# Seven tile products for eight in two of eight row-tile pairs of the plain down products, with weight chunks of 2048

## The chip, the cores and the metric

The kernel runs on one core of a Trainium2 chip. The metric is the device time of one execution in microseconds (us); the profile gives, for one execution of its own, the span from the first to the last instruction of the core.

## The reference

The reference is a decoder trunk of two layers on 256 tokens of 2048 features in float32. Layer 0 mixes tokens by a causal pooling mixer, layer 1 by a dilated attention with three head groups; each layer ends with a squared-relu MLP, and each of the four sublayers with a scaled residual and a layer norm:

```python
for i in range(DEPTH):                       # DEPTH = 2
    if i % N_MIXERS == 0: h = pool_mixer(x, ...)
    else:                 h = dilated_attention(x, ...)
    x = layer_norm(DEEPNORM_ALPHA * x + h, ln_mix_g[i], ln_mix_b[i])
    x = layer_norm(DEEPNORM_ALPHA * x + sqrelu_mlp(x, mlp_w_up[i], mlp_w_down[i]), ln_mlp_g[i], ln_mlp_b[i])

def sqrelu_mlp(x, w_up, w_down):             # w_up 2048 x 8192, w_down 8192 x 2048
    h = jax.nn.relu(x @ w_up)
    return (h * h) @ w_down
```

The two MLPs hold most of the work. In the kernel each product is made of three matmuls on parts of reduced width: high times high, high times low and low times high.

## The kernel before

**Weights.** All weights are planned as one list of chunks in the order of use; a chunk is 128 rows by 1024 columns (`CHUNK`). `load` (L116) gives each chunk one of 4 `raw` buffers (`RAWS`) and a DMA on SP's queue. `prefetch` (L129) then splits it by `split_from` (L61): ACT copies the high part `wh` (L62), DVE subtracts it to make `wl` (L63). A split pair sits in one of 8 buffers (`SPLITS`) until TensorE (PE) has used it. A raw buffer is free for the next DMA when DVE has made `wl`. `weights()` (L140) takes the next pair and first writes the splits of the chunks up to 8 ahead into the programs of ACT and DVE. The programs of PE, DVE and ACT are in the order in which the code is written, and each engine goes through its own in order; SP does too, and runs ahead as raws come free.

**The MLP** (L520) goes in four parts c of 2048 hidden columns. A part first makes its hidden columns in *up blocks* (`feature_major`, L186) of 512 columns, four a part (in c=0 the first is split in two of 256 columns, made by `opening` while the norm is being finished, and one block of 256). A block of 512 uses 8 chunks and four of the 8 PSUM banks, one for each 128 columns. The *hidden chain* then works on each pair of banks: ACT copies the low half out (`low`, L230), DVE adds (`u`, L231), ACT takes relu (L531) and square (L533) and makes `hH`, DVE makes `hL` (L63). Eight hidden pairs `hs[0]` to `hs[7]`, of two row tiles each, are the left operand of the part's *down products*. Parts c=0 to 2 are *plain*: four groups of 512 output columns, each by `token_major` (L248) in two banks, one for each of the two token tiles t, then added to the residual `xz` (L569, L571). Part c=3 is a `closing`, which makes the norm's moments, transposes the result and lets the next `opening` begin.

In c=0, `drain()` puts a *restore* behind a block: four DVE instructions (L352, L353) that apply the norm's gain and bias to `xz`, and the DMAs of the next rows `gb`, which POOL issues (L346).

**Start.** The pooling mixer's first product, w_in, goes in four blocks n=0 to 3 of 512 columns; behind each the windows are summed (`win`, `pv`) and split to `pT`. While n=0 runs, ACT and DVE also split the transposed input `xT`, and `feature_major` prefetches less far ahead (L195).

Of the kernel before, what the change touches and what calls it, by code (L numbers as in the profile page):

```python
# [9 lines left out]
F32 = mybir.dt.float32  # L10
# [3 lines left out]
OP = mybir.AluOpType  # L14
# [18 lines left out]
MASKED = -1e30  # L33
CHUNK = 1024
RAWS = 4
SPLITS = 8
RESIDENT = 4
MLP_PARTS = 4
UP_FIRST = (256, 256, 512, 512, 512)
UP_REST = (512, 512, 512, 512)  # L40
# [6 lines left out]
def trunk(ctx: ExitStack, tc: tile.TileContext, x, pool_w_in, pool_w_group, pool_scale, pool_w_out,  # L47
# [27 lines left out]

    def plan(w, k0, nk, n0, ncols):
        step = CHUNK // ncols
        for k in range(k0, k0 + nk, step):
            chunks.append((w[:, k:k + step, n0:n0 + ncols], step, ncols))

    def plan_columns(w, k0, nk, n0, widths):
        for ncols in widths:
            plan(w, k0, nk, n0, ncols)
            n0 += ncols

    def plan_mlp(l):
        for c in range(MLP_PARTS):
            plan_columns(w_up[l], 0, KT, c * D, UP_FIRST if c == 0 else UP_REST)
            plan_columns(w_down[l], c * KT, KT, 0, CLOSING if c == MLP_PARTS - 1 else UP_REST)

# [3 lines left out]
    def plan_values(sp):  # L94

        w_v = w_qkv.rearrange("p k (y g n) -> p k y g n", y=3, g=GROUPS)
        for k in range(0, KT, 2):
            chunks.append((w_v[:, k:k + 2, 2, 1:3, sp * 256:(sp + 1) * 256], 2, 512))

    plan_columns(w_in, 0, KT, 0, UP_REST)  # L100
    for g in range(4):
# [9 lines left out]
    plan_mlp(1)  # L111

    raws, ready = [], []
    state = {"raw": 0, "split": 0, "used": 0}

    def load(upto):  # L116

        while state["raw"] < min(upto, len(chunks)):
            src, step, ncols = chunks[state["raw"]]
            raw = wraw.tile([P, step, ncols], F32, tag="raw", name="raw")  # L120
            if len(src.shape) == 4:
                for j in range(step):
                    nc.sync.dma_start(raw[:, j, :].rearrange("p (g n) -> p g n", g=src.shape[2]), src[:, j])
            else:
                nc.sync.dma_start(raw, src)
            raws.append(raw)
            state["raw"] += 1

    def prefetch(upto):  # L129

        while state["split"] < min(upto, len(chunks)):
            load(state["split"] + 1)
            _, step, ncols = chunks[state["split"]]
            hi = wsplit.tile([P, step, ncols], F32R, tag="wh", name="wh")
            lo = wsplit.tile([P, step, ncols], F32R, tag="wl", name="wl")
            split_from(hi, lo, raws.pop(0))
            ready.append((hi, lo))
# [127 lines left out]
    def tile_products(ps, t, nk, parts, act, start=True, between=()):  # L265

        k = 0
        for i, (hi, lo) in enumerate(parts):
# [7 lines left out]
            k += step  # L276


    class Norm:
        def __init__(self, g, b, cidx, last=None):  # L280
# [58 lines left out]
        def restores(self):  # L339
# [18 lines left out]
            return [lambda n=n: restore(n) for n in range(NG)]  # L358

        def centre(self, t, ns):  # L360
            for n in ns:
                z = xz[:, t, n * 512:(n + 1) * 512]
                nc.vector.scalar_tensor_tensor(z, z, self.mv[t][:, 0:1], self.last[:, 0, n * 512:(n + 1) * 512],
                                               op0=OP.subtract, op1=OP.mult)

        def output(self, t, ns):
            for n in ns:
                sl = slice(n * 512, (n + 1) * 512)
                z = xz[:, t, sl]
# [66 lines left out]
    def opening(norm, ncols):  # L436
# [83 lines left out]
    def mlp(norm_in, norm):  # L520
        with ExitStack() as ph:
            hp = ph.enter_context(tc.tile_pool(name="hp", bufs=8))
            hb = ph.enter_context(tc.tile_pool(name="hb", bufs=2))
            if norm.last is not None:
                for i, v in enumerate((norm.g, norm.b)):
                    nc.gpsimd.dma_start(norm.last[:, i, :], v[None, :].to_broadcast([P, D]))

            def hidden(ps):
# [7 lines left out]
            def split_hidden(q):  # L536
# [3 lines left out]
                return hH, hL  # L540

            for c in range(MLP_PARTS):
                hs = []
# [19 lines left out]
                if c < MLP_PARTS - 1:  # L563
                    for n in range(NG):
                        ps = token_major(KT, 512, act)
                        for t in range(NT):
                            z = xz[:, t, n * 512:(n + 1) * 512]
                            if c == 0:
                                nc.vector.scalar_tensor_tensor(z, z, ALPHA, ps[t], op0=OP.mult, op1=OP.add)  # L569
                            else:  # L570
                                nc.vector.tensor_add(z, z, ps[t])  # L571
                else:
# [7 lines left out]
    with ExitStack() as ph:  # L580
# [127 lines left out]
        for sp in range(SLOTS // 2):  # L708
# [69 lines left out]
```

## Time and profile before

| | us |
|---|---|
| median of three runs | 2146.16 (2145.59 to 2147.05) |
| the profiled execution | 2146.52 |
| span of the profiled execution | 2144.7 |
| TensorE (PE) busy | 2124.7 (99%) |
| VectorE (DVE) busy | 1283.4 (60%) |
| ScalarE (ACT) busy | 1052.8 (49%) |

Some 1.8 us of the profiled execution lie outside its span. A busy share is an average over stages; PE is busy nearly throughout, so what counts for the time is how many matmuls it has and whether their operands and banks are ready.

### The profile page before, as it was taken

How to read it: one execution, taken by the hardware profiler on the slowest of the kernel's cores; microseconds unless marked ns; L12 is line 12 of the kernel's file. 1: busy time of each engine (PE TensorE's matmuls, PEld its weight loads, DVE VectorE, ACT ScalarE, POOL GpSimd, SP SyncE). 2: the span in 40 equal slices, each digit the busy share in tenths (PEclk: the TensorE clock that was granted, in tenths of full speed). 3: DMA queues.
4: the chain of work that ended last, by engine and by line, in shares of the span. 5: the costliest groups of instructions: out<-in, count | busy, mean ns of one | idle time of the engine just before them, and what ended most of it. 6: DMA issues, size and time to landing. Idle time of an engine off the chain costs nothing.

```text
span 2144.7 us, 29773 instructions
## 1 busy us (share of the span) xinstructions
PE 2124.7 (99%) x11745; PEld 1845.9 (86%) x11745; DVE 1283.4 (60%) x1558; ACT 1052.8 (49%) x1368; POOL 23.0 (1%) x52
## 2 busy tenths in 40 slices
PE   8999999999999999999999999999999999999998
PEld 7889888888888888898998988888888888888887
DVE  6785756555455555578656565676655555554555
ACT  4563655454355355354545444455545534644541
POOL 1000000000000000001000000000000000000000
PEclk9999999999999999999999999999999999999999
DMA  7565567556655655548555555456665566566562
GB/s 239 204 216 177 169 204 237 175 199 201 191 185 196 194 172 206 194 139 237 173 175 161 176 162 173 164 164 218 209 221 178 201 197 188 176 207 186 181 207 94
DMA packets 256045, 404.67 MB, mean 189 GB/s; under 512 B 13104, under 2 KB 109984, under 8 KB 255648
## 3 DMA queue, kind: packets, MB, share of 16 engines
q1 hardware_dynamic: 253472, 394.31, 56.7%
q0 software_dynamic: 2432, 8.45, 1.9%
q8 instruction: 92, 1.51, 0.3%
q14 instruction: 49, 0.40, 0.1%
HBM read 400.61 MB, written 2.10 MB: 188 GB/s over the span
## 4 chain that ended last, share of the span: by engine, by line
PE 96%; DVE 2%; DMA 1%; ACT 1%; issue 0%; SPq 0%; DVEq 0%; ACTq 0%
PE pt L245 45%; PE pf L202 32%; PE pf L204 16%; PE pf L221 1%; PE pq L658 1%; PE po L697 1%; DMA raw<-in_attn_w_qkv 0%; DVE wl L63 0%; PE ptr L321 0%; DMA xz<-in_x 0%; ACT xv L330 0%; DVE xT L337 0%; DVE vL L63 0%; PE ptr L458 0%; DVE xT L336 0%
## 5 line engine op out<-in xcount | busy, mean ns | idle before, releaser
L63 DVE TENSOR_TENSOR wl<-raw,wh 128x1024 fp32r<-128x1024 f32 x744 | 898.2, 1224 | 621.1 <-ACT wh L62 607.1
L62 ACT ACTIVATE wh<-raw 128x1024 fp32r<-128x1024 f32 x744 | 773.4, 1057 | 805.8 <-PE pt L245 351.4
L202 PE MATMUL pf<-xT,wh 128*128 128x512 f32 x3008 | 947.6, 396 | 0.0
L204 PEld LDWEIGHTS pf<-xT,wl 128*128 128x128 f32 x3008 | 566.0, 188 | 134.0 <-DVE wl L63 0.6
L204 PE MATMUL pf<-xT,wl 128*128 128x256 f32 x3008 | 592.2, 278 | 0.0
L202 PEld LDWEIGHTS pf<-xT,wh 128*128 128x128 f32 x3008 | 459.5, 189 | 0.5
L245 PE MATMUL pt<-wl,hH 128*128 128x512 f32 (+1 forms) x1088 | 407.0, 377 | 0.0
L245 PE MATMUL pt<-wh,hH 128*128 128x512 f32 (+1 forms) x1088 | 407.0, 377 | 0.0
L245 PE MATMUL pt<-wh,hL 128*128 128x512 f32 (+1 forms) x1088 | 398.2, 377 | 0.0
L245 PEld LDWEIGHTS pt<-wl,hH 128*128 128x128 f32 x1088 | 204.8, 188 | 37.6 <-DVE wl L63 0.4
L245 PEld LDWEIGHTS pt<-wh,hH 128*128 128x128 f32 x1088 | 204.8, 188 | 37.5
L245 PEld LDWEIGHTS pt<-wh,hL 128*128 128x128 f32 x1088 | 199.6, 188 | 37.1
L245 PE MATMUL pt<-wh,xT 128*128 128x256 f32 (+1 forms) x704 | 156.4, 314 | 1.9 <-DVE xT L336 1.5
L245 PEld LDWEIGHTS pt<-wh,xT 128*128 128x128 f32 x704 | 117.2, 191 | 10.6 <-DVE xT L336 3.1
L63 DVE TENSOR_TENSOR hL<-q,hH 128x512 fp32r<-128x512 f32 x62 | 42.9, 693 | 125.6 <-ACT hH L62 125.6
L245 PE MATMUL pt<-wl,xT 128*128 128x256 f32 (+1 forms) x352 | 106.7, 312 | 0.0
L230 ACT ACTIVATE low<-pf 128x256 f32<-128x256 f32 x188 | 61.3, 377 | 69.6 <-PE pf L204 62.7
L245 PE MATMUL pt<-wh,pT 128*128 128x512 f32 (+1 forms) x320 | 82.6, 347 | 0.0
L231 DVE TENSOR_TENSOR u<-pf,low 128x256 f32<-128x256 f32 x172 | 64.7, 418 | 26.0 <-ACT low L230 26.0
L245 PEld LDWEIGHTS pt<-wl,xT 128*128 128x128 f32 x352 | 67.2, 191 | 3.6
L531 ACT ACTIVATE r<-u 128x512 f32<-128x512 f32 x62 | 39.2, 632 | 51.0 <-DVE u L231 51.0
L245 PEld LDWEIGHTS pt<-wh,pT 128*128 128x128 f32 x320 | 56.1, 189 | 7.5
(126 smaller groups left out, 1001.8 us busy)
## 6 DMA issues: line engine op xcount, KB each, us to landing
raw<-in_mlp_w_up SPq DMA_DIRECT2D x256, 512.0 KB, 4.4
raw<-in_mlp_w_down SPq DMA_DIRECT2D x256, 512.0 KB, 4.5
raw<-in_attn_w_qkv SPq DMA_DIRECT2D x120, 512.0 KB, 4.3
raw<-in_pool_w_in SPq DMA_DIRECT2D x32, 512.0 KB, 5.4
raw<-in_pool_w_out SPq DMA_DIRECT2D x32, 512.0 KB, 4.7
raw<-in_attn_w_qkv SPq DMA_DIRECT2D x48, 256.0 KB, 3.3
raw<-in_attn_w_out SPq DMA_DIRECT2D x16, 512.0 KB, 4.4
raw<-in_pool_w_group SPq DMA_DIRECT2D x8, 512.0 KB, 5.0
```

The source lines that it names most:

```text
L62: nc.scalar.activation(hi, src, AF.Copy)
L63: nc.vector.tensor_sub(lo, src, hi.bitcast(F32))
L202: nc.tensor.matmul(ps[b], hi[:, j, sl], a, start=(k == 0), stop=False, skip_group_check=True)
L204: nc.tensor.matmul(ps[b][:, 0, :], lo[:, j, sl], a[:, 0, :], start=False, stop=(k == nk - 1), skip_group_check=True)
L221: nc.tensor.matmul(ps[b // 2][:, b % 2, :], w[:, j, sl], a[:, part, :], start=(k == 0 and i == 0 and b % 2 == 0), stop=(k == nk - 1 and i ...
L230: nc.scalar.activation(low, p[:, 1, :], AF.Copy)
L231: nc.vector.tensor_add(out[:, b, :], p[:, 0, :], low)
L245: nc.tensor.matmul(ps, a[:, sl], u, start=(start and k == 0 and i == 0), stop=(k == nk - 1 and i == 2), skip_group_check=True)
L531: nc.scalar.activation(r, ps, AF.Relu)
L658: nc.tensor.matmul(pq[:, t, :], q[u][:, b, sl], k[v][:, b, :], start=(i == 0), stop=(i == 2))
L697: nc.tensor.matmul(po, v[:, st, b * P:(b + 1) * P], p[:, g, sl], start=(i == 0), stop=(i == 3 * 2 * GROUPS - 1))
```

## The change

Two of the eight pairs of row tiles (hidden pairs 1 and 4, `SEVEN`) of each plain part are multiplied by a scheme of seven tile products where two tokens tiles times two row tiles times two column halves want eight. It needs sums of the weight's tiles (`split_seven`), sums of the hidden pair's tiles (`split_seven_left`) and sums of the products (`sums`). A plain part's down products now go in two groups of 1024 columns, with all 8 banks (`mixed_group`). Chunks are 2048 columns, with 2 raws, 4 split buffers and 2 resident chunks, which is the same memory. With chunks twice as long, the places that stand "before the last chunk" (the transposes in `closing` and `opening`) and the prefetch at the start move; `drain()` stands ahead of a block, the last norm's rows come by SP through raw buffers, and in the attention one set of transposes (not shown) stands ahead of the last value chunk.

```diff
-CHUNK = 1024
-RAWS = 4
-SPLITS = 8
-RESIDENT = 4
+CHUNK = 2048
+RAWS = 2
+SPLITS = 4
+RESIDENT = 2
+MIX = (1, 0, 2, 4, 3, 5, 6, 7)
+SEVEN = (1, 4)
...
+    def split_seven(raw):
+        q = raw.rearrange("p k (h n) -> p (k h) n", h=2)
+        t = state["diff"].tile([P, 4, 512], F32, tag="t", name="t")
+        nc.vector.tensor_sub(t[:, 0:2], q[:, 1:3], q[:, 0:1].to_broadcast([P, 2, 512]))
+        nc.vector.tensor_add(t[:, 2], q[:, 2], t[:, 0])
+        nc.vector.tensor_sub(t[:, 3], q[:, 3], t[:, 2])
+        plain, sums = split_buffers([P, 4, 512]), split_buffers([P, 4, 512])
+        split_from(plain[0][:, 1:], plain[1][:, 1:], q[:, 1:])
+        split_from(sums[0], sums[1], t)
...
-            hi, lo = weights(SPLITS if start_up is None else min(2 + kc // 4, SPLITS))
+            hi, lo = weights(SPLITS if start_up is None else 1 + kc // 8)
             for j in range(kstep):
                 k = kc + j
+                if start_up is not None and j == 2:
+                    start_up(k)
+                    lookahead(1)
...
+    def mixed_group(act, left_factors, z, first):
+        names = ("P1", "P5", "P7", "P6", "P2", "P3", "P4", "P0")
+        ps = {name: bank([P, 512], "pt") for name in names}
...
+        def sums():
+            one, two, three = (tmp.tile([P, 512], F32, tag="xv", name="us", bufs=3) for _ in range(3))
+            nc.scalar.activation(one, ps["P1"], AF.Copy)
+            nc.vector.tensor_add(two, ps["P6"], one)
+            add(0, 1, ps["P1"], True)
+            nc.vector.tensor_add(three, ps["P7"], two)
+            nc.vector.tensor_add(two, ps["P5"], two)
+            add(1, 1, three, True)
+            nc.vector.tensor_add(three, ps["P5"], three)
+            add(0, 0, two, True)
+            add(1, 0, three, True)
+        last_seven = max(MIX.index(i) for i in SEVEN)
+        for n, i in enumerate(MIX):
+            a, b = 2 * i, 2 * i + 1
+            if i in SEVEN:
+                w, f = weights(), left_factors[i]
+                for name, left, right in (("P1", tokens(a, 0), "B11"), ("P5", f(0), "T1"), ("P7", f(2), "T3"),
+                                          ("P6", f(1), "T2"), ("P2", tokens(b, 0), "B21"), ("P3", f(3), "B22"),
+                                          ("P4", tokens(b, 1), "T4")):
+                    product(name, left, w[right], n == last_seven and name in ("P1", "P5", "P7", "P6"))
+            else:
+                hi, lo = weights()
+                for j, k in enumerate((a, b)):
+                    for name, t, h in (("P2", 0, 1), ("P3", 0, 0), ("P4", 1, 1), ("P0", 1, 0)):
...
+            if n == last_seven + 1:
+                sums()
+        add(0, 1, ps["P2"])
+        add(0, 0, ps["P3"])
+        add(1, 1, ps["P4"])
+        add(1, 0, ps["P0"])
...
-        prefetch(state["used"] + 2)
+        lookahead(1)
         tile_products(both[:, 1, :], 1, KT, parts, x_parts, start=False)
...
+            def split_seven_left(q):
+                (a11, a21), (a12, a22) = ((q[:, i, :P], q[:, i, P:]) for i in range(2))
+                d = hb.tile([P, 4, P], F32, tag="r", name="d")
...
+                dH = dp.tile([P, 4, P], F32R, tag="dH", name="dH")
+                dL = dp.tile([P, 4, P], F32R, tag="dL", name="dL")
+                split_from(dH, dL, d)
...
                 for ncols in UP_FIRST[1:] if c == 0 else UP_REST:
+                    drain()
                     ps = feature_major(KT, ncols, x_act)
...
-                        hs.append(split_hidden(hidden(u)))
-                    drain()
+                        q = hidden(u)
+                        if c < MLP_PARTS - 1 and len(hs) in SEVEN:
+                            left_factors[len(hs)] = split_seven_left(q)
+                        hs.append(split_hidden(q))
```

A product is three matmuls of 128x512. A group of 1024 columns had 8 pairs x 8 products x 3 = 192 of them and now has (6 x 8 + 2 x 7) x 3 = 186; twelve such groups make 72 fewer.

Of ACT's program, the place between the blocks n=0 and n=1 of w_in at the start is shown first, as it was; `low`, `pT` and what they work on belong to n=0, `xT` to its input, and `wh` are weights.

```order
L62 ACTIVATE xT<-ptr 128x2x256
L62 ACTIVATE wh<-raw 128x1024 x3
L230 ACTIVATE low<-pf 128x256 x4
L62 ACTIVATE pT<-pv 128x4x256
L62 ACTIVATE wh<-raw 128x1024 x11
```

This is the same place in ACT's program now.

```order
L66 ACTIVATE wh<-raw 128x1024 x2
L66 ACTIVATE xT<-ptr 128x2x256 x2
L66 ACTIVATE wh<-raw 128x2048
L294 ACTIVATE low<-pf 128x256 x4
L66 ACTIVATE pT<-pv 128x4x256
L66 ACTIVATE wh<-raw 128x2048 x6
```

Ahead of `low`, twelve chunks of 1024 columns were split, of which n=0 uses eight; now eight pieces of 1024 columns and one chunk of 2048 are, so that n=1 finds one quarter of its weights split ahead of `pT` where it found half.

Of DVE's program, this is the end of the up blocks of part c=1 in the kernel before, with its first group of down products.

```order
L231 TENSOR_TENSOR u<-pf,low 128x256 x2
L63 TENSOR_TENSOR hL<-q,hH 128x512
L231 TENSOR_TENSOR u<-pf,low 128x256 x2
L63 TENSOR_TENSOR hL<-q,hH 128x512
L63 TENSOR_TENSOR wl<-raw,wh 128x1024 x8
L571 TENSOR_TENSOR xz<-xz,pt 128x512 x2
```

The same place now reads as follows; `t` are sums of weight tiles.

```order
L295 TENSOR_TENSOR u<-pf,low 128x256 x2
L67 TENSOR_TENSOR hL<-q,hH 128x512
L67 TENSOR_TENSOR wl<-raw,wh 128x2048
L164 TENSOR_TENSOR t<-raw 128x1024
L165 TENSOR_TENSOR t<-raw,t 128x512
L166 TENSOR_TENSOR t<-raw,t 128x512
L67 TENSOR_TENSOR wl<-raw,wh 128x1536
L67 TENSOR_TENSOR wl<-t,wh 128x2048
L67 TENSOR_TENSOR wl<-raw,wh 128x2048 x4
L370 TENSOR_TENSOR us<-pt,us 128x512
L365 TENSOR_TENSOR xz<-xz,pt 128x512
```

The eight instructions of `sums` begin behind the weights of the pairs that end the group. The rows that follow lead from the first group of the part into the second.

```order
L372 TENSOR_TENSOR us<-pt,us 128x512
L373 TENSOR_TENSOR us<-pt,us 128x512
L365 TENSOR_TENSOR xz<-xz,us 128x512
L375 TENSOR_TENSOR us<-pt,us 128x512
L365 TENSOR_TENSOR xz<-xz,us 128x512 x2
L164 TENSOR_TENSOR t<-raw 128x1024
L165 TENSOR_TENSOR t<-raw,t 128x512
L166 TENSOR_TENSOR t<-raw,t 128x512
L67 TENSOR_TENSOR wl<-raw,wh 128x1536
L67 TENSOR_TENSOR wl<-t,wh 128x2048
L67 TENSOR_TENSOR wl<-raw,wh 128x2048
L365 TENSOR_TENSOR xz<-xz,pt 128x512 x4
```

The weights with which the second group begins now stand behind the first group's sums, and its four last adds to `xz` behind two chunks of the second group.

## Rows read from the trace of the kernel before

**Rows 1.** The page: busy time, share of the span and instructions of each engine.
```profile
PE 2124.7 (99%) x11745; PEld 1845.9 (86%) x11745; DVE 1283.4 (60%) x1558; ACT 1052.8 (49%) x1368; POOL 23.0 (1%) x52
```
**Rows 2.** The page: the chain of work that ended last, by engine.
```profile
PE 96%; DVE 2%; DMA 1%; ACT 1%; issue 0%; SPq 0%; DVEq 0%; ACTq 0%
```
**Rows 3.** Pieces of that chain: start, us, what (two stretches of time).
```profile
8.78 0.85 PE pf L202 x2
...
305.72 0.47 PE pf L202 x2
...
308.50 87.33 PE pt L245 x384
```
**Rows 4.** Groups by form: line, engine, out<-in, count | busy, mean ns | idle before.
```profile
L63 DVE TENSOR_TENSOR wl<-raw,wh 128x1024 fp32r<-128x1024 f32 x744 | 898.2, 1224 | 621.1 <-ACT wh L62 607.1 <-PE pf L204 6.5 <-PE pf L202 2.0
...
L63 DVE TENSOR_TENSOR hL<-q,hH 128x512 fp32r<-128x512 f32 x62 | 42.9, 693 | 125.6 <-ACT hH L62 125.6
L571 DVE TENSOR_TENSOR xz<-xz,pt 128x512 f32<-128x512 f32 x32 | 20.5, 682 | 0.0
...
L353 DVE TENSOR_TENSOR xz<-xz,gb 128x512 f32<-128x512 f32 x24 | 16.6, 692 | 0.8
...
L661 DVE SCALAR_TENSOR_TENSOR sc<-dist,pq 128x128 f32<-128x128 f32 x24 | 6.7, 280 | 0.0
...
L62 ACT ACTIVATE wh<-raw 128x1024 fp32r<-128x1024 f32 x744 | 773.4, 1057 | 805.8 <-PE pt L245 351.4 <-PE pf L202 198.2 <-DMA raw<-in_mlp_w_down 111.3
...
L62 ACT ACTIVATE hH<-q 128x512 fp32r<-128x512 f32 x62 | 39.2, 632 | 2.0
```
**Rows 5.** DMA issues of the whole span: count, KB each, median us to landing.
```profile
raw<-in_mlp_w_up SPq DMA_DIRECT2D x256, 512.0 KB, 4.4
...
raw<-in_attn_w_qkv SPq DMA_DIRECT2D x48, 256.0 KB, 3.3
...
last<-in_ln_mlp_g POOLq DMA_DIRECT2D x1, 1024.0 KB, 4.8
last<-in_ln_mlp_b POOLq DMA_DIRECT2D x1, 1024.0 KB, 6.8
```
**Rows 6.** Line L125, which issues the weights' DMAs: all of its landings.
```profile
DMA to landing us min/median/max: 3.2/4.4/9.4
```
**Rows 7.** DMA issues of 279 to 283 us (c=0), then of 426.0 to 426.2 us (c=1).
```profile
raw<-in_mlp_w_up SPq DMA_DIRECT2D x4, 512.0 KB, 7.4
...
raw<-in_mlp_w_up SPq DMA_DIRECT2D x1, 512.0 KB, 3.6
```
**Rows 8.** DVE in order of time, hidden chains of c=1: start, us, ..., [idle before].
```profile
417.76 0.76 DVE L231 TENSOR_TENSOR u<-pf,low 128x256 f32<-128x256 f32 x2 [0.30 <-ACT low L230]
...
421.15 0.75 DVE L231 TENSOR_TENSOR u<-pf,low 128x256 f32<-128x256 f32 x2
423.93 0.69 DVE L63 TENSOR_TENSOR hL<-q,hH 128x512 fp32r<-128x512 f32 x1 [2.03 <-ACT hH L62]
...
440.05 0.76 DVE L231 TENSOR_TENSOR u<-pf,low 128x256 f32<-128x256 f32 x2 [0.30 <-ACT low L230]
```
**Rows 9.** ACT in order of time: `low` of three blocks of c=0, then c=1.
```profile
267.34 0.64 ACT L230 ACTIVATE low<-pf 128x256 f32<-128x256 f32 x2
...
291.44 0.64 ACT L230 ACTIVATE low<-pf 128x256 f32<-128x256 f32 x2
...
315.79 0.64 ACT L230 ACTIVATE low<-pf 128x256 f32<-128x256 f32 x2
...
417.34 0.66 ACT L230 ACTIVATE low<-pf 128x256 f32<-128x256 f32 x2 [1.14 <-PE pf L204]
...
423.80 1.99 ACT L62 ACTIVATE wh<-raw 128x1024 fp32r<-128x1024 f32 x2
```
**Rows 10.** ACT in order of time, between n=0 and n=1 of w_in.
```profile
34.98 0.66 ACT L230 ACTIVATE low<-pf 128x256 f32<-128x256 f32 x2 [1.33 <-PE pf L204]
...
44.41 2.94 ACT L62 ACTIVATE wh<-raw 128x1024 fp32r<-128x1024 f32 x3
```
**Rows 11.** A stretch: busy time (instructions) of each engine, PEclk, DMA share, GB/s.
```profile
12.50:20.00 7.50, 7.50 (x48) 6.71 (x48) 3.76 (x4) 4.04 (x5) 0.00 (x0) 1.00 1.03 383
```
**Rows 12.** PE in order of time, at the end of the first closing.
```profile
217.55 0.39 PE L245 MATMUL pt<-wh,xT 128*128 128x256 f32 x1 [0.24 <-DVE xT L336]
```
**Rows 13.** The waits: us in total, times, longest us.
```profile
ACT wh L62 <- DMA raw<-in_mlp_w_down: 111.3, 72, 8.2
...
PEld po L697 <- DVE PTL L63: 1.5, 3, 0.5
```

More of the change, by code (lines that the diff above doesn't have):

```diff
@@ L84, in plan_columns, with plan_mixed @@
             n0 += ncols
+    def plan_mixed(w, k0, n0):
+        for i in MIX:
+            k = k0 + 2 * i
+            if i in SEVEN:
+                chunks.append((w[:, k:k + 2, n0:n0 + WIDE], 2, WIDE, 2, 1))
+            else:
+                plan(w, k, 2, n0, WIDE)
     def plan_mlp(l):
@@ L88, in plan_mlp @@
             plan_columns(w_up[l], 0, KT, c * D, UP_FIRST if c == 0 else UP_REST)
-            plan_columns(w_down[l], c * KT, KT, 0, CLOSING if c == MLP_PARTS - 1 else UP_REST)
+            if c == MLP_PARTS - 1:
+                plan_columns(w_down[l], c * KT, KT, 0, CLOSING)
+            else:
+                for n0 in range(0, D, WIDE):
+                    plan_mixed(w_down[l], c * KT, n0)
     def qkv_col(sp, ty, g):
@@ L96, in plan_values @@
         w_v = w_qkv.rearrange("p k (y g n) -> p k y g n", y=3, g=GROUPS)
[L97 to L100 removed]
+        for k in range(0, KT, 4):
+            chunks.append((w_v[:, k:k + 4, 2, 1:3, sp * 256:(sp + 1) * 256], 4, 512, 1, 1))
+    plan(w_in, 0, KT, 0, 512, 2)
+    plan_columns(w_in, 0, KT, 512, UP_REST[1:])
     for g in range(4):
@@ L111, in trunk, with load @@
     plan_mlp(1)
+    begins = [0]
+    for c in chunks:
+        begins.append(begins[-1] + c[3])
     raws, ready = [], []
     state = {"raw": 0, "split": 0, "used": 0}
-    def load(upto):
+    def load(upto, between=()):
         while state["raw"] < min(upto, len(chunks)):
-            src, step, ncols = chunks[state["raw"]]
+            src, step, ncols, _, pieces = chunks[state["raw"]]
             raw = wraw.tile([P, step, ncols], F32, tag="raw", name="raw")
@@ L124, in load, with split_buffers @@
             else:
-                nc.sync.dma_start(raw, src)
+                n = step // pieces
+                for j in range(0, step, n):
+                    nc.sync.dma_start(raw[:, j:j + n], src[:, j:j + n])
+                    if between and j + n < step:
+                        between.pop(0)()
             raws.append(raw)
             state["raw"] += 1
+    def split_buffers(shape):
+        return [wsplit.tile(shape, F32R, tag="w" + x, name="w" + x) for x in "hl"]
+    def split_seven(raw):
[7 more added lines that the diff above has]
+        split_from(sums[0], sums[1], t)
+        return {name: (x[0][:, i], x[1][:, i]) for name, x, i in (
+            ("B11", plain, 1), ("B22", plain, 2), ("B21", plain, 3),
+            ("T1", sums, 0), ("T3", sums, 1), ("T2", sums, 2), ("T4", sums, 3))}
@@ L129, in prefetch @@
     def prefetch(upto):
-        while state["split"] < min(upto, len(chunks)):
+        while state["split"] < len(chunks) and begins[state["split"] + 1] <= upto:
             load(state["split"] + 1)
[L133 to L137, printed above, removed]
+            _, step, ncols, units, pieces = chunks[state["split"]]
+            raw = raws.pop(0)
+            if units > 1:
+                ready.append(split_seven(raw))
+            else:
+                hi, lo = split_buffers([P, step, ncols])
+                n = step // pieces
+                for j in range(0, step, n):
+                    split_from(hi[:, j:j + n], lo[:, j:j + n], raw[:, j:j + n])
+                ready.append((hi, lo))
@@ L138, in prefetch, with lookahead @@
             state["split"] += 1
+    def lookahead(n):
+        prefetch(begins[state["used"]] + n)
     def weights(ahead=SPLITS):
-        prefetch(state["used"] + max(ahead, 1))
+        lookahead(max(ahead, 1))
         state["used"] += 1
@@ L358, in restores, with rows_of_last, row @@
             return [lambda n=n: restore(n) for n in range(NG)]
+        def rows_of_last(self):
+            self.rows = []
+            for v in (self.g, self.b):
+                self.rows.append(wraw.tile([P, D], F32, tag="raw", name="row"))
+                nc.sync.dma_start(self.rows[-1], v[None, :].to_broadcast([P, D]))
+        def row(self, i, n):
+            return self.rows[i][:, n * 512:(n + 1) * 512]
         def centre(self, t, ns):
@@ L374, in closing @@
     def closing(nk, act, first, norm, before_last=None):
-        held = RESIDENT if norm.last is None else SPLITS
+        held = RESIDENT if not norm.last else SPLITS
         nres = held * CHUNK // (nk * CLOSING[-1])
@@ L383, in closing @@
         per = nk * CLOSING[-1] // CHUNK
-        prefetch(state["used"] + SPLITS)
+        lookahead(SPLITS)
         parts = resident(held)
+        if norm.last:
+            norm.rows_of_last()
         def tile_end(t, between=()):
@@ L401, in closing @@
         norm.moments(0)
-        if norm.last is not None:
+        if norm.last:
             norm.centre(0, [0])
@@ L523, in mlp @@
             hb = ph.enter_context(tc.tile_pool(name="hb", bufs=2))
-            if norm.last is not None:
-                for i, v in enumerate((norm.g, norm.b)):
-                    nc.gpsimd.dma_start(norm.last[:, i, :], v[None, :].to_broadcast([P, D]))
+            dp = ph.enter_context(tc.tile_pool(name="dp", bufs=len(SEVEN)))
+            state["diff"] = ph.enter_context(tc.tile_pool(name="wdiff", bufs=1))
             def hidden(ps):
@@ L563, in mlp @@
                 if c < MLP_PARTS - 1:
[L564 to L571, printed above, removed]
+                    for n0 in range(0, D, WIDE):
+                        mixed_group(act, left_factors,
+                                    lambda t, h: xz[:, t, n0 + h * 512:n0 + (h + 1) * 512], c == 0)
                 else:
```

64 lines of the change are left out of this document (47 added, 17 removed).

## The prediction

> **What bounds the kernel now.** I read the page first: PE is busy for 99% of the span [rows 1], and the chain of work that ended last runs on PE for 96% of it [rows 2]. In the pieces of that chain one plain part's down products are a single piece of 384 matmuls in 87.33 us [rows 3]: 0.2274 us each, with no gap. So each 128x512 matmul taken out is worth 0.2274 us, and each delay that reaches PE costs its whole length. What has to be asked is how far the supply (DMA, ACT's `wh`, DVE's `wl`) is ahead of PE, and whether the change keeps that lead.
>
> I read it from the timelines. In c=1 the first `u` of two successive blocks starts at 417.76 and at 440.05 [rows 8], so a block takes PE 22.3 us. A hidden chain lasts from the first `low` at 417.34 [rows 9] to the end of the last `hL` at 423.93 + 0.69 = 424.62 [rows 8]: 7.3 us, in which DVE splits no weights, since it goes in order. In c=0 the first `low` of three successive blocks comes at 267.34, 291.44 and 315.79 [rows 9]: 24.2 us apart, so the chain of supply falls behind PE by 1.9 us a block there. What c=0 adds is a restore, 4 x 0.69 = 2.8 us of DVE [rows 4], and landings of 7.4 us instead of the usual 4.4, with the `gb` rows in the way [rows 5, 7]: some 2.6 more. So 5.4 us of extra work cost 1.9, and **a block of the kernel before has 3.4 us to spare**. It lives on a lead that ends with c=0; the waits for `w_down` DMAs of up to 8.2 us [rows 13] are of that kind, and none reaches PE.
>
> **Part by part.**
>
> *Removed:* 72 matmuls x 0.2274 = **-16.4 us**. The Trainium skill, "TensorE: Matmul & The Clock Gate", section "Back-to-back issue gap", gives some 131 ns as the sustained spacing of matmuls of 512 columns, by which the removed ones would be worth 9.4 us. The trace disagrees: 0.2274 us over 384 of them [rows 3].
>
> *Prices of the new sizes.* `wl` takes 1.224 us for 1024 columns and a subtraction of 512 takes 0.693 [rows 4], so 512 columns more cost 0.53: 2.29 for 2048, 1.76 for 1536. `wh` takes 1.057 and 0.632 [rows 4]: 1.91 for 2048. The landing M of a 1024 KB chunk isn't in the trace. One row has that size: 4.8 us, and 6.8 for the second behind it [rows 5]. The first of a train of 512 KB landed after 3.6 [rows 7], and at 383 GB/s [rows 11] a further 512 KB takes 1.37: 4.95. I take **M = 4.9**. Below, the shortest landing, 3.2 [rows 6], plus 1.37 gives 4.55; above, the median 4.4 [rows 5] plus 1.37 and a little queueing gives 5.9. (256 KB to 512 KB raises the median from 3.3 to 4.4 [rows 5]; carried on, that would be 6.6.) The Trainium skill, "DMA: Bandwidth & Descriptors", section "Anatomy of one DMA — SWDGE (gpsimd) path", fits a DMA as about 2.0 us plus its bytes at 436 GB/s, an estimate of 4.4 us here. By it the sum below would be some 15 us smaller; the only row of this size, 4.8, is longer.
>
> *An up block with two raws.* Let h be the end of a hidden chain, when both raws A and B are full. `wh` of A began with the end of `hH` (423.80 against 424.62 before [rows 8, 9]), so `wl` of A ends at h+3.5 and that of B at h+5.8. Only then are their raws loaded again: C lands at h+3.5+M and is split by h+7.7+M, D by h+10.05+M. The next hidden chain stands behind D on DVE and takes 7.3. The cycle is 17.35+M = 22.25 against PE's 22.3: **the 3.4 us to spare become nothing.** PE doesn't stop for that by itself: A is the last quarter of the running block, needed 16.7 us after its start and ready after 7.3+3.5 = 10.8, so the supply may be 5.9 us late.
>
> *Parts c=1, 2 (four in all).* The left factors of pair 1 (four 0.28 us operations and a 0.63 us `dH` [rows 4], with handovers 1.85) make the chain 1.85 late for the rest of the part; those of pair 4 fall beside ACT's relu of the pair behind it. A mixed group wants all 8 banks at once. The last block's are freed by `u`: P2's is needed 12 matmuls (2.7 us) into the group; `low`, `u` and handovers take 1.0 of that, so of the 1.85 some 0.2 reach PE; P4's is freed 3.4 us behind it (417.76 to 421.15 [rows 8]) where PE needs it 1.4 behind: 2.0. The chunk of pair 2 is split behind the hidden chain and the seven-sums behind it (2.6 + 1.76 + 2.29): about 1.1 together. At the boundary of the two groups, the first group's `sums` (8 x 0.68 = 5.4 [rows 4]) stand on DVE behind the `wl` of pairs 5 to 7, whose three DMAs go two at a time: `sums` begin about 35.0 us into the group and end at 40.4; then t 2.6, `wl` 1.76 and 2.29 make the second group's B and T weights ready at 47.3, where PE wants T1's low part at 42.3 + 1.0 plus the 2.2 already lost: 1.8. P2's bank comes by an add behind the next 2048-column `wl`: another 1.2. Sum: 0.2 + 2.0 + 1.1 + 1.8 + 1.2 = 6.3, four times **+25**.
>
> *Parts c=0 (two).* Each block adds 2.8 of restore and 2.6 of `gb` landing to a chain with nothing to spare. With the left factors the first 512-column block is 7.2 late, over the 5.9 by 1.3; the two behind it could each add 5.4 more. I count 10 for the three, since a PE that waits lets the `gb` rows land in its own wait; then, fully late at the down products, 3.9 for the banks and T1's low part, 1.1 and 3.0 as above: 18 a part, **+36** (13 a part if the `gb` rows cost nothing).
>
> *Start-up.* n=1 now finds one quarter of its weights split. n=0 ends about 35.7 (its first `low` starts at 34.98, the other two banks 0.7 later [rows 10]); a quarter lasts 5.6, to 41.3. The next `wh` stands behind `pT` and starts at 44.41 [rows 10]; +1.91, and `wl` +2.29, makes 48.65, with one pair of matmuls (0.47 [rows 3]) in between: **+7**. PE's first pair after its idle start took 0.85 instead of 0.47 [rows 3], so up to 2 more. The pooling blocks behind it have the same window chain with two raws: between 0 and 7, I take **+3**.
>
> *Closings and attention.* Transposes now stand ahead of 24 instead of 36 matmuls of 256 columns, some 1.4 us less cover, three times; the first closing already waits 0.24 for `xT` [rows 12]: 0 to 4. The attention's waits for `PTL`, 1.5 in three [rows 13], may go. Net **+1**. The last norm's rows on SP cost nothing, hidden behind the last closing's own products; uncovered, two landings of 4.8.
>
> **Sum:** -16.4 + 7 + 3 + 1 + 25 + 36 = +56, on the profiled execution's 2146.5 (0.4 above the median): **2202 us**. At M = 4.55 each part with c>0 costs 4.4 and each c=0 16, so 2190; at M = 5.9 the cycle is 1.0 over each block, 12 and 24, so 2238.
>
> **The rivals.**
> 1. *The raws keep up* (the other side). If 1024 KB land in 3.2 us, as single 512 KB chunks sometimes did [rows 6], the cycle is 20.55 and 1.75 are spare; left factors and boundary are covered, c>0 parts cost 0.5 each and, if the `gb` rows no longer delay two raws, c=0 parts 1 each. With 7 at the start and nothing in the pooling blocks: -16.4 + 7 + 1 + 2 + 2 = -4, **2142**; with nothing lost at all, 2130. It decides below M of about 3.3. Against it: no row of 1024 KB is under 4.8. For it: fewer transfers share the queues.
> 2. *Only the boundaries cost.* If c=0 is no worse than c>0, since the restores now stand ahead of the block: -16.4 + 11 + 6 x 6.3 = +32, **2179**. Against it: 2.8 us of restore have no place in a chain with nothing to spare.
> 3. *Landings are those of a loaded queue*, M = 5.9: **2238**, and by 6.6 over 2260. For it: trains of two always follow each other, as the 6.8 does [rows 5].
> 4. *Landings of a lightly used queue*, M = 4.55: **2190**, as worked out above. For it: the 3.2 [rows 6]; against it: the 4.8 [rows 5]. Of the pages named above, the one on DMA points to this rival, and the one on TensorE to 7 us more than the forecast.
>
> **How the numbers follow.** Forecast (2195 to 2225) 0.38; first rival 0.17; second (2160 to 2183) 0.14; third 0.16; fourth (2183 to 2195) 0.15. The forecast with the fourth, the likeliest pair, runs from 2183 to 2225. The measurement tells apart about 0.2%, 4.3 us. Of the first rival 0.12 lies below 2142 and 0.05 within 4.3 us of before. The range that leaves two in ten out runs from 2142 to 2240. Faster 0.12, same 0.05, slower 0.83.
>
> **What would show it.** In the changed profile: 72 fewer matmuls at 0.227; a gap of some 7 us on PE near 41 to 49 us; raws landing near 4.9; in c=1, 2 PE gaps at the begin of each first group and at each second group, 6 us a part, and none in the up blocks; in c=0 gaps in the blocks' last quarter too. Wrong would be: landings under 4, c=1 free of gaps, or PE gaps at places not named here.

## The result and the profile after

The changed kernel takes **2233.5 us** (median of 4 runs, 2231.6 to 2234.6) against 2146.6 before: 1.040 times, with a 95% interval of 1.039 to 1.042. The forecast was 2202 with a range of 2142 to 2240. The profiled execution has a span of 2232.6 us and a mean granted clock of 0.987, against 0.999 before.

The page of the changed kernel: the engines' busy time, and the chain that ended last.
```profile
PE 2142.9 (96%) x11673; PEld 1842.7 (83%) x11673; DVE 1411.7 (63%) x1442; ACT 1033.7 (46%) x1048; POOL 23.1 (1%) x50
...
PE 48%; DVE 20%; DMA 14%; ACT 12%; issue 5%; ACTq 0%; DVEq 0%; SPq 0%
```
There are 72 fewer records of matmuls [rows 1]. PE had 96% of the chain [rows 2]; now half of it is DVE, DMA and ACT: for half of the span the supply decides when PE can go on, though PE is still busy for 96% of it.

Groups by form, the new sizes of DVE and ACT.
```profile
L67 DVE TENSOR_TENSOR wl<-raw,wh 128x2048 fp32r<-128x2048 f32 x344 | 785.7, 2291 | 558.1 <-ACT wh L66 543.6 <-PE pf L266 6.8 <-PE pf L268 6.7
L66 ACT ACTIVATE wh<-raw 128x2048 fp32r<-128x2048 f32 x344 | 655.5, 1913 | 703.2 <-DMA raw<-in_mlp_w_up 271.3 <-DMA raw<-in_mlp_w_down 198.7 <-DMA raw<-in_attn_w_qkv 48.4
...
L67 DVE TENSOR_TENSOR wl<-raw,wh 128x1536 fp32r<-128x1536 f32 x24 | 42.0, 1751 | 0.0
```
2.29, 1.91 and 1.75 us: the prices that the prediction carried on from [rows 4] hold to 0.01. What ACT waits for has changed: chiefly PE before, now the DMAs.

DMA issues of the changed kernel, first from 434 to 523 us (up blocks of c=1), then from 259.7 to 342 us (up blocks of c=0).
```profile
raw<-in_mlp_w_up SPq DMA_DIRECT2D x12, 1024.0 KB, 5.1
...
raw<-in_mlp_w_up SPq DMA_DIRECT2D x9, 1024.0 KB, 6.2
...
gb<-in_ln_mix_b POOLq DMA_DIRECT2D x2, 256.0 KB, 5.9
```
A 1024 KB chunk lands after 5.1 us in c=1, where no `gb` rows travel, and after 6.2 in c=0, where they do.

PE in order of time, some of its waits: the start, the pooling mixer's group products, c=0, c=1, the opening of the attention.
```profile
45.93 1.22 PE L266 MATMUL pf<-xT,wh 128*128 128x512 f32 x2 [4.89 <-ACT wh L66]
48.26 0.80 PE L268 MATMUL pf<-xT,wl 128*128 128x256 f32 x2 [1.10 <-DVE wl L67]
...
132.79 0.50 PE L285 MATMUL pf<-pT,wh 128*128 128x256 f32 x2 [2.61 <-ACT wh L66]
135.12 0.43 PE L285 MATMUL pf<-pT,wl 128*128 128x256 f32 x1 [1.82 <-DVE wl L67]
...
280.22 0.51 PE L268 MATMUL pf<-xT,wl 128*128 128x256 f32 x2 [3.12 <-DVE wl L67]
...
306.49 0.79 PE L268 MATMUL pf<-xT,wl 128*128 128x256 f32 x2 [2.78 <-DVE wl L67]
...
334.31 0.80 PE L268 MATMUL pf<-xT,wl 128*128 128x256 f32 x2 [3.05 <-DVE wl L67]
...
526.88 0.50 PE L353 MATMUL pt<-wh,hH 128*128 128x512 f32 x1 [0.70 <-DVE u L295]
530.26 0.50 PE L353 MATMUL pt<-wh,hH 128*128 128x512 f32 x1 [1.73 <-DVE u L295]
543.64 0.50 PE L353 MATMUL pt<-wl,dH 128*128 128x512 f32 x1 [0.51 <-DVE wl L67]
571.78 0.50 PE L353 MATMUL pt<-wl,dH 128*128 128x512 f32 x1 [1.32 <-DVE wl L67]
574.58 0.50 PE L353 MATMUL pt<-wh,hH 128*128 128x512 f32 x1 [0.68 <-DVE xz L365]
...
1023.81 0.80 PE L268 MATMUL pf<-xT,wl 128*128 128x256 f32 x2 [4.10 <-DVE wl L67]
```
Each row shows who was late. In c=1 these are the places of the prediction: P2's and P4's banks at the start of the first group (`u`), the chunk of pair 4 (`wl`), and at 571.78 the second group's first T weights and a bank that an add (`xz`) had still to free. At 45.93 and 48.26 are the two waits of the start, forecast for 46.3 and 48.65.

Stretches of the changed kernel: busy time of PE, PEld, DVE, ACT, POOL, then PEclk, DMA share, GB/s.
```profile
45.00:49.00 4.00, 1.97 (x5) 1.25 (x6) 3.43 (x3) 2.68 (x2) 0.00 (x0) 0.50 0.00 0
49.00:54.00 5.00, 5.00 (x19) 4.25 (x18) 1.40 (x1) 0.00 (x0) 0.00 (x0) 0.56 0.96 305
54.00:60.00 6.00, 6.00 (x37) 5.25 (x36) 2.75 (x2) 3.84 (x2) 0.00 (x0) 1.00 0.26 98
259.70:342.20 82.50, 72.29 (x387) 61.54 (x386) 49.56 (x54) 38.09 (x42) 3.19 (x6) 0.94 0.57 183
434.00:523.00 89.00, 89.00 (x513) 77.64 (x513) 50.99 (x51) 46.14 (x49) 0.00 (x0) 1.00 0.53 175
```
The up blocks of c=1 are free of gaps, as forecast (those of c=2 in layer 0 have one wait, 0.65 us at 699.06). At the end of the wait of the start the granted clock is 0.50 (the lower level, 1.2 GHz) and PE, though busy all of the next 5 us, gets 0.56; so this wait cost more than its length. In c=0 the mean is 0.94.

Where the time went, from the start of the first matmul of each stage in PE's order of time (us; the spans of the profiled executions; the rows below the first two are experiments). A c=0 part counts from its first up block of 512 columns; the blocks of 256 columns ahead of it stand in the columns before it.

| kernel | start, pooling | w_out to first block of 512 | both c=0 | c=1, 2 of both layers | c=3, attention, opening | last c=3 | span |
|---|---|---|---|---|---|---|---|
| before | 125.6 | 115.8 | 308.4 | 704.8 | 701.9 | 188.2 | 2144.7 |
| changed | 142.2 | 117.5 | 347.0 | 726.5 | 711.5 | 187.9 | 2232.6 |
| chunk size alone | 147.7 | 117.4 | 336.1 | 704.8 | 710.2 | 188.2 | 2204.4 |
| changed, eight products | 142.5 | 117.4 | 331.9 | 704.9 | 709.2 | 187.9 | 2193.8 |
| changed, third raw | 141.9 | 117.4 | 321.4 | 696.5 | 711.9 | 187.9 | 2177.0 |
| changed, no `gb` DMAs | 141.9 | 117.4 | 336.5 | 728.6 | 712.2 | 187.9 | 2224.5 |
| changed, longer look-ahead | 137.5 | 117.4 | 346.2 | 731.7 | 709.4 | 187.9 | 2230.1 |
| changed, halves | 132.3 | 116.6 | 322.2 | 694.5 | 701.8 | 188.3 | 2155.7 |
| scheme, chunks of 1024 | 126.3 | 115.8 | 326.0 | 694.0 | 701.8 | 188.0 | 2151.9 |
| the same, restores on POOL | 125.6 | 118.1 | 312.8 | 694.0 | 714.1 | 188.1 | 2152.6 |
| the scheme in c=1, 2 alone | 125.9 | 115.8 | 308.8 | 694.1 | 701.3 | 188.0 | 2133.9 |

A part has 12 matmuls less, 2.7 us; so c=0 lost 38.6 + 5.5 = 44 us, and c=1, 2 lost 21.7 + 10.9 = 33. The kernels without `gb` DMAs and with the longer look-ahead run the same program in c=1, 2 as the changed one, and took 2 and 5 us more there; the 33 is known no better than that.

### The profile page after: what moved, and what is told of

Read it like the earlier page. It is cut to its first block, busy times and chain, and to the rows that moved or that the text cites. A ratio compares the mean times of both kernels' runs of the same rounds, so it can differ in the third digit from the quotient of the medians.

```text
span 2232.6 us, 27714 instructions
## 1 busy us (share of the span) xinstructions
PE 2142.9 (96%) x11673; PEld 1842.7 (83%) x11673; DVE 1411.7 (63%) x1442; ACT 1033.7 (46%) x1048; POOL 23.1 (1%) x50
## 4 chain that ended last, share of the span: by engine, by line
PE 48%; DVE 20%; DMA 14%; ACT 12%; issue 5%; ACTq 0%; DVEq 0%; SPq 0%
PE pf L266 16%; PE pt L309 13%; DVE wl L67 10%; PE pt L353 9%; PE pf L268 8%; ACT wh L66 8%; DMA raw<-in_mlp_w_up 6%; DMA raw<-in_mlp_w_down 6%; DVE u L295 1%; DMA raw<-in_attn_w_qkv 1%; ACT q L666 1%; ACT r L664 1%; PE pq L802 1%; PE po L841 1%; DVE xz L365 1%
## 5 line engine op out<-in xcount | busy, mean ns | idle before, releaser
L67 DVE TENSOR_TENSOR wl<-raw,wh 128x2048 fp32r<-128x2048 f32 (+2 forms) x376 | 837.3, 2234 | 561.7 <-ACT wh L66 547.3
L66 ACT ACTIVATE wh<-raw 128x2048 fp32r<-128x2048 f32 (+2 forms) x376 | 698.1, 1867 | 742.5 <-DMA raw<-in_mlp_w_up 271.3
L353 PE MATMUL pt<-wh,hH 128*128 128x512 f32 x648 | 255.2, 394 | 20.4 <-DVE u L295 16.4
L353 PE MATMUL pt<-wl,hH 128*128 128x512 f32 x648 | 253.5, 391 | 0.0
L353 PE MATMUL pt<-wh,hL 128*128 128x512 f32 x648 | 253.0, 390 | 0.0
L353 PEld LDWEIGHTS pt<-wh,hH 128*128 128x128 f32 x648 | 122.1, 188 | 53.0 <-DVE u L295 21.7
L353 PEld LDWEIGHTS pt<-wl,hH 128*128 128x128 f32 x648 | 122.2, 189 | 25.7 <-DVE wl L67 1.1
L309 PE MATMUL pt<-wh,hH 128*128 128x512 f32 (+1 forms) x320 | 107.4, 347 | 0.0
L309 PE MATMUL pt<-wl,hH 128*128 128x512 f32 (+1 forms) x320 | 107.3, 347 | 0.0
L309 PE MATMUL pt<-wh,hL 128*128 128x512 f32 (+1 forms) x320 | 97.2, 347 | 0.0
```

The costliest lines, as they stand in the source:

```text
L66: nc.scalar.activation(hi, src, AF.Copy)
L67: nc.vector.tensor_sub(lo, src, hi.bitcast(F32))
L309: nc.tensor.matmul(ps, a[:, sl], u, start=(start and k == 0 and i == 0), stop=(k == nk - 1 and i == 2), skip_group_check=True)
L353: nc.tensor.matmul(ps[name], a[u], w[v], start=(name not in begun), stop=(last and i == 2), skip_group_check=True)
```

## The experiments

The theory: two raws of 2048 columns take too long from release to split, so that the supply has nothing to spare, and all that is late in it (restores, left factors, sums, window chains) reaches PE. Its rival: the sevenfold scheme itself (its sums, its adds, its eight banks at once) makes the loss.

**Chunk size alone** (the kernel before):
```diff
-CHUNK = 1024
-RAWS = 4
-SPLITS = 8
-RESIDENT = 4
+CHUNK = 2048
+RAWS = 2
+SPLITS = 4
+RESIDENT = 2
...
-            hi, lo = weights(SPLITS if start_up is None else min(2 + kc // 4, SPLITS))
+            hi, lo = weights(SPLITS if start_up is None else 1 + kc // 8)
...
```


> The kernel before with chunks of 2048, 2 raws, 4 split buffers, 2 resident chunks and the shorter look-ahead of the start; no sevenfold scheme. If the loss comes from two raws of double size: the start and the pooling blocks lose 15 us as in the changed kernel, the up blocks of c=0 about 14 in each layer, the attention 8, the plain groups of 512 columns little: about 2200. If the scheme itself (sums, adds, eight banks) makes the loss: under 2160.

Measured: 2207.7 (ratio 1.029, 1.027 to 1.030). The chunk size, with the look-ahead of the start that belongs to it, makes some 61 of the 87 us without a single seven-product; c=1, 2 lose nothing by it (704.8 in the table).

**The scheme alone, with chunks of 1024:** a seven-pair comes in two raws and is split in four pairs of buffers; the restores stay where the changed kernel has them.
```diff
...
+        nc.vector.tensor_sub(t[:, 0], q1, q0)
+        nc.vector.tensor_sub(t[:, 1], q2, q0)
+        nc.vector.tensor_add(t[:, 2], q2, t[:, 0])
+        nc.vector.tensor_sub(t[:, 3], q3, t[:, 2])
+        one, s01, s23, two = (split_buffers([P, 2, 512]) for _ in range(4))
...
```


> The scheme alone, with the chunks of 1024, the 4 raws and the start of the kernel before; the weights of a seven-pair come in two raws. If the loss comes from the raws: 16.4 us gained, less the waits for banks (P4's 1.9) and perhaps 1 to 3 at the boundary in each of six parts: 2138 to 2150. If the scheme itself makes the loss, six parts at 6 to 7 us of waits stay: about 2170.

Measured: 2156.4 (1.0042, 1.0027 to 1.0057), between the two expectations. The table decides by stage: c=1, 2 gain their whole 10.8 us, so there the scheme costs nothing; c=0 loses 17.6 us where 5.5 were to be gained. PE in order of time at the end of c=0's up blocks, the waits:
```profile
310.55 0.80 PE L279 MATMUL pf<-xT,wl 128*128 128x256 f32 x2 [2.84 <-DVE wl L67]
320.83 0.50 PE L364 MATMUL pt<-wh,hH 128*128 128x512 f32 x1 [2.11 <-DVE u L306]
324.21 0.50 PE L364 MATMUL pt<-wh,hH 128*128 128x512 f32 x1 [1.73 <-DVE u L306]
```
The kernel before falls behind in c=0 as well [rows 9], at no cost: a plain group takes two banks that are free. A group that wants all eight passes the lateness on. The banks are not all of it: the wait at 310.55 is for a `wl` in the up block ahead of the group, and the chain there now has the left factors too.

**The changed kernel with eight products:**
```diff
-SEVEN = (1, 4)
+SEVEN = ()
...
-        names = ("P1", "P5", "P7", "P6", "P2", "P3", "P4", "P0")
+        names = ("P2", "P3", "P4", "P0")
...
```


> The changed kernel with all eight pairs by eight products (192 matmuls a group again), no sums, no left factors, four banks a group. If the raws make the loss: 16.4 back, the gaps in the groups gone (about 6.5 in each of six parts), the up blocks of c=0 a little better: 2205 to 2212. If the scheme makes it: about 2150.

Measured: 2194.5 (1.0219, 1.0204 to 1.0234), 10 us below what was expected if the raws make the loss. With 16.4 us of matmuls more it is 39 us faster than the changed kernel: on two raws the scheme costs 55 us. So neither cause stands alone.

**A third raw in the MLPs:**
```diff
+            pool = state["third"] if state.get("third") and state["raw"] % 3 == 2 else wraw
...
+            state["third"] = ph.enter_context(tc.tile_pool(name="wthird", bufs=1))
...
```


> The changed kernel with a third raw buffer of 2048 columns inside the MLPs (u and q with one buffer each to make room). If the time that a raw needs to be loaded again makes the loss, the up blocks of c=0 lose under 6 us a layer instead of 17 and the boundaries of the groups most of their 2.4: about 2190. If DVE's own work is the limit, nothing changes: 2228 or more.

Measured: 2178.5 (1.0145, 1.013 to 1.016), with one buffer less for each of `u` and `q`. c=1, 2 fall from 726.5 to 696.5, 2.6 above what the removed matmuls allow; c=0 loses 18.5 instead of 44. The DMAs didn't get faster (5.4 from issue to landing in the up blocks of c=1, x10); there is one more buffer to be waiting in.

**Without the `gb` DMAs:**
```diff
+                if n > 0:
+                    gbs[n] = gbs[0]
+                    return
```


> The changed kernel without the gb DMAs behind the first of each norm; every restore then applies the gain and bias of the first 512 columns, so the norm's gain and bias of the other columns are left out. If the gb rows delay the weights by 2.6 us a block, the up blocks of c=0 lose about 17 - 7 us a layer and the opening of the attention 3 less: about 2210. If only DVE's restores count: 2229 or more.

Measured: 2225.8 (1.0367, 1.0352 to 1.0382), 8 us less than the changed kernel where 23 were expected. In c=0 alone it is 10.5 us (336.5 for 347.0); c=1, 2 and the attention came out 2.8 longer. So the `gb` rows make about a quarter of c=0's 44. DMA issues of this kernel, from 259.3 to 334.7 us (up blocks of c=0):
```profile
raw<-in_mlp_w_up SPq DMA_DIRECT2D x9, 1024.0 KB, 5.2
```
With the `gb` rows it was 6.2: 1.0 us a landing.

**A longer look-ahead at the start** (the changed kernel):
```diff
-            hi, lo = weights(SPLITS if start_up is None else 1 + kc // 8)
+            hi, lo = weights(SPLITS if start_up is None else 1 + kc // 4)
```


> The changed kernel with a look-ahead of 1 + kc // 4 chunks in the first block, so that three chunks of n=1 are split ahead of pT. If the order of splits behind pT makes the wait at the start, the 7.2 us of gap and 2 us of slow matmuls behind it go: about 2224. If the raws are too late anyway, they stay or move into n=0: 2230 or more.

Measured: 2234.0 (1.041, 1.039 to 1.043), no gain. The waits at 46 and 48 us are gone, but `xT` is split behind the weights now, and n=1 begins at 41.2 instead of 35.2. Up to w_out 4.7 us came back all the same (137.5 for 142.2), and c=1, 2, in which nothing was changed, took 5.2 more; why is not shown. PE in order of time:
```profile
32.68 1.22 PE L266 MATMUL pf<-xT,wh 128*128 128x512 f32 x2 [2.58 <-DVE xT L67]
```

**Three ways around c=0's lateness** (the scheme with chunks of 1024). First, the group begins with a plain pair on the free banks:
```diff
-MIX = (1, 0, 2, 4, 3, 5, 6, 7)
+MIX = (0, 1, 2, 4, 3, 5, 6, 7)
...
-        names = ("P1", "P5", "P7", "P6", "P2", "P3", "P4", "P0")
+        names = ("P2", "P3", "P4", "P0", "P1", "P5", "P7", "P6")
```


> The scheme with chunks of 1024 as run above, but a group begins with a plain pair, whose four products take the four banks that are free, and a seven-pair follows. If the waits for banks alone cost the 4.2 us behind the up blocks of c=0: 4 us less in each layer, 2148. If DVE is simply late there, the wait moves to the next weights: 2153 or more.

Measured: 2154.3 (1.0036, 1.0023 to 1.0049): about as without it. The wait for `u` only comes three microseconds later (3.82 us). Second, two restores go into the down group:
```diff
+            if first and n in (2, 6):
+                drain()
...
-                    drain()
...
+                    if b < 2:
+                        drain()
```


> The scheme with chunks of 1024 as run above, with two of the four restores of c=0 moved behind the third and the seventh pair of the first down group. If the restores and their gb rows make c=0 late, the gaps of about 7.5 us a layer and the slow matmuls behind them go: about 2138. If the scheme's bank waits are there without lateness, 2150 or more.

Measured: 2154.5 (1.0033, 1.0021 to 1.0045). The wait in the up blocks is gone, and came back: PE in order of time,
```profile
313.04 0.50 PE L364 MATMUL pt<-wh,hH 128*128 128x512 f32 x1 [2.71 <-DVE u L306]
...
362.55 0.58 PE L364 MATMUL pt<-wh,hH 128*128 128x512 f32 x1 [5.04 <-DVE xz L376]
```
the second restore stands ahead of the adds that free the next group's banks. Third, POOL computes the restores:
```diff
-                    nc.vector.tensor_mul(z, z, gbs[n][:, 0, :])
-                    nc.vector.tensor_add(z, z, gbs[n][:, 1, :])
+                    nc.gpsimd.tensor_mul(z, z, gbs[n][:, 0, :])
+                    nc.gpsimd.tensor_add(z, z, gbs[n][:, 1, :])
```


> The scheme with chunks of 1024 as run above, with the restores computed by POOL instead of DVE (2.8 us of DVE less a block in c=0 and in the attention's opening). If DVE's restores are what makes c=0 late, its gaps of about 8 us a layer go to under 2: 2133 to 2140, faster than before. If the gb DMAs alone make it late, or POOL's work slows DVE: 2148 or more.

Measured: 2156.8 (1.0044, 1.0030 to 1.0058). The two c=0 parts take 312.8 instead of 326.0: of the 23.1 us that they lose (17.6, and 5.5 for the removed matmuls) 13.2 go with the restores on DVE. But the attention and the closings ahead of it take 714.1 instead of 701.8. DVE, then POOL, over the same time (the opening ahead of c=0):
```profile
229.41 0.69 DVE L472 TENSOR_TENSOR xT<-xv,xT 128x512 fp32r<-128x512 f32 x1
230.01 4.55 DVE L67 TENSOR_TENSOR wl<-raw,wh 128x1024 fp32r<-128x1024 f32 x2
234.72 6.60 DVE L67 TENSOR_TENSOR wl<-raw,wh 128x1024 fp32r<-128x1024 f32 x4
```
```profile
229.81 3.68 POOL L487 TENSOR_TENSOR xz<-xz,gb 128x512 f32<-128x512 f32 x2 [2.84 <-DMA gb<-in_ln_mix_g]
233.44 4.52 POOL L488 TENSOR_TENSOR xz<-xz,gb 128x512 f32<-128x512 f32 x2
```
Two `wl` take 4.55 us where two took 2.35 without POOL.

**Halves of a chunk** (the changed kernel): each plain chunk by two DMAs, split in two.
```diff
-    def plan(w, k0, nk, n0, ncols, pieces=1):
+    def plan(w, k0, nk, n0, ncols, pieces=2):
```


> The changed kernel with every chunk of 2048 loaded by two DMAs of 512 KB and split in two halves (seven-pairs and the attention's values as they are); the buffers stay two of 2048. If the time from a raw's release to its split, and not the bytes, makes the loss, a cycle gets shorter by about 2.2 us (first half lands 1.4 earlier, the first wh is 0.85 shorter), for 0.2 us more of work a chunk: about 2200. If bandwidth or DVE's work is the limit: 2233 or more.

Measured: 2159.3 (1.0055, 1.0041 to 1.0068). Same buffers, same bytes, 74 us less, more than twice what was expected; why so much more is not shown. DMA issues of this kernel, from 409.8 to 499 us (up blocks of c=1):
```profile
raw<-in_mlp_w_up SPq DMA_DIRECT2D x23, 512.0 KB, 4.5
```
ACT in order of time, the two halves of one chunk in c=1:
```profile
446.94 1.06 ACT L66 ACTIVATE wh<-raw 128x1024 fp32r<-128x1024 f32 x1 [3.56 <-DMA raw<-in_mlp_w_up]
448.25 1.06 ACT L66 ACTIVATE wh<-raw 128x1024 fp32r<-128x1024 f32 x1 [0.25 <-DMA raw<-in_mlp_w_up]
```
It isn't bandwidth: the first half's split begins while the second half still lands. From the release of this raw to the end of its next split it is 7.6 us, and 9.5 at the same place of the changed kernel.

**The scheme where there is no lateness:** chunks of 1024, seven-products in c=1, 2 alone, c=0 as before.
```diff
...
+                    if c == 0 and n0 < PLAIN:
+                        plan_columns(w_down[l][:, :, n0:n0 + WIDE], 0, KT, 0, (512, 512))
+                    else:
+                        plan_mixed(w_down[l], c * KT, n0)
...
```


> The scheme with chunks of 1024 in parts c=1 and 2 alone; c=0 has the plain groups of 512 columns and the place of the restores of the kernel before. If the loss left in the scheme with small chunks is c=0's lateness, which a group with all eight banks passes on to TensorE, nothing is lost and 48 matmuls are gone: 10.9 us less, 2134 to 2138. If the scheme costs in every part: 2146 or more.

Measured: **2135.7 (0.9945, 0.9932 to 0.9957)**, faster than both kernels by more than the measurement's doubt. Page of this kernel:
```profile
PE 2113.5 (99%) x11697; PEld 1836.1 (86%) x11697; DVE 1396.2 (65%) x1758; ACT 1084.7 (51%) x1416; POOL 22.0 (1%) x50
```
With c=0's second 1024 columns by the scheme too (`PLAIN` 1024 instead of 2048):

> The same, and in c=0 the second 1024 columns by the scheme as well (its first 1024 plain). If the two plain groups give DVE the time to catch up, 60 matmuls are gone and little is lost: 13.6 us less, 2132 to 2136. If c=0's lateness lasts to its second half, or its left factors make it later: 2138 or more.

Measured: 2140.2 (0.9966, 0.9952 to 0.9979): 12 matmuls less and 4.5 us more. c=0's lateness lasts into its down products. In its second plain group PE waits for a `wl`, and on DVE the last restore of the up blocks stands ahead of that `wl`:
```profile
332.19 0.50 PE L324 MATMUL pt<-wl,hH 128*128 128x512 f32 x1 [2.45 <-DVE wl L68]
```
```profile
328.26 0.69 DVE L491 TENSOR_TENSOR xz<-xz,gb 128x512 f32<-128x512 f32 x1
...
330.92 4.62 DVE L68 TENSOR_TENSOR wl<-raw,wh 128x1024 fp32r<-128x1024 f32 x4
```
Counted from its start, c=0 reaches that restore after 85.8 us; in the run before this one, without left factors in c=0, after 82.9, and the same wait is 0.38 there. So left factors, ahead of groups that take two banks, make c=0 late enough to reach PE.

## Why the prediction was right, and where its sizes were off

- *The supply has nothing to spare on two raws:* right, and shown from both sides. A third raw takes 55 us off and halves 74, with the scheme and the sizes of the chunks in place. M was 5.1 in c=1, not 4.9. The Trainium skill, "DMA: Bandwidth & Descriptors", section "Anatomy of one DMA — SWDGE (gpsimd) path", whose fit gave an estimate of 4.4, lies under what this queue showed.
- *Removed, -16.4:* right. In c=1, 2 without lateness (chunks of 1024) 48 matmuls less gave 10.8 us, 0.225 each; the 131 ns of the Trainium skill, "TensorE: Matmul & The Clock Gate", section "Back-to-back issue gap", is not what these matmuls cost.
- *Parts c=1, 2, +25:* measured 33. The waits stand at the forecast places; c=1 of layer 0 lost 7.1 (its down products, from 522.8 to 614.2, take 4.4 longer than before, and 2.7 were removed) where 6.3 were worked out; the other three lost 7.5 to 9.7.
- *Parts c=0, +36:* measured 44. Lateness from restores and from `gb` landings was the right mechanism. In the up blocks of layer 0 PE was idle for 10.2 of 82.5 us, where 10 were counted. The `gb` share fits too: 18 a part, 13 without them, makes 10 for both, and 10.5 came back. Their price was not right: the rows give 3.0 us (7.4 less 4.4) where the text says 2.6, and 1.0 was measured. The 23 expected of the run without them were more than the prediction's own working gives. Left out was the clock, 0.94 over the up blocks: 82.5 us at 0.94 are, as an estimate, some 5 us a layer.
- *Start and pooling, +10:* measured 16.6. The two waits came at the forecast times, 6.0 us together; the half-speed matmuls behind them were named as "up to 2 more" and not counted. The pooling stage cost some 7, not 3, and not where the text put it: the blocks n=2 and n=3 have one wait of 0.9, the group products behind them the two at 132.79 and 135.12, 4.4 us.
- *Closings and attention, +1:* this term failed. It measured 11.0 (1.7 + 9.6 - 0.3). Some 7 of it fall on the attention's first projections, from 990 to 1068 us, where PE waits 4.10 us at 1023.81 for a `wl`; the text treated the attention only under waits for `PTL`. On DVE a restore, as in c=0, and behind it the distances for the attention's masks (`dist`, 5.4 us) stand ahead of that `wl`:
```profile
1013.45 0.68 DVE L475 TENSOR_TENSOR xz<-xz,gb 128x512 f32<-128x512 f32 x1
...
1016.11 0.36 DVE L746 TENSOR_SCALAR dist<-scratch 128x128 f32<-128x128 int32 x2
...
1021.47 4.68 DVE L67 TENSOR_TENSOR wl<-raw,wh 128x2048 fp32r<-128x2048 f32 x2
```
The `gb` rows are not the cause here: without them the column is 712.2, against 711.5. With halves it is 701.8, as before: with more lead the same work no longer reaches PE.
- *The signs of being wrong:* landings and c=1 came out as forecast, but two places with gaps were not named, the pooling group products and the attention's opening.
- *The rivals:* the raws didn't keep up (first); c=0 was not like c>0 (second: 44 against 33 over half as many parts). M = 5.9 (third, 2238) gives nearly the measured time by the wrong cause: landings were 5.1 (6.2 in c=0 alone), and the 31 us above the forecast are the terms above. 2233.5 lies outside the forecast's own 2195 to 2225; that the range held it, by the room left for the third rival, is in part luck.

What stays open: how the part of c=0's 44 us that is not `gb` divides between restores, left factors, banks and clock. In the scheme with chunks of 1024 the restores on DVE account for 13 of 23.

## What to carry to other kernels

Before buffers are merged into fewer and larger ones, work out the cycle of one buffer (release, landing, split, and what stands ahead of the split on its engine) against the time in which the consumer uses it up; equal bytes are not equal lead. Loading and splitting a large buffer in halves gave 74 of the 87 us back here. Work that a lead has hidden for nothing, such as a late engine in front of two free banks, can become a wait as soon as the next stage wants all banks at once: save such a scheme for the stages that arrive on time.

## What the runs showed of the hardware

DVE and POOL, both on 128-partition elementwise work, held each other up: `wl` of 1024 columns went from 1.22 us to 2.3 while POOL multiplied (4.55 us for two), and a 128x512 product on POOL, 1.29 us where DVE was idle, took 1.84 beside it (3.68 for two); 48 instructions of 0.69 us, 33 us in all, went from DVE to POOL, and DVE was busy for 1458.9 us instead of 1453.8. And a wait of PE of some 5 us was followed by a stretch at a granted clock of 0.50 to 0.56, with 19 records of matmuls in 5 us against 37 in the 6 us behind it.
